# A hybrid diffusion step on one core: key halves copied by DMA, prompt steps and the last query turn moved, two small loads issued elsewhere

## The chip, the core and the metric

The kernel runs on one core of one Trainium2 chip. It is one program with five instruction streams: TensorE (PE, with its weight loads as PEld), VectorE (DVE), ScalarE (ACT), GpSimd (POOL) and SyncE (SP), which only issues DMAs here; ACT issues some DMAs too. Each stream runs in its own order, and streams wait for each other by semaphores. The metric is the device time of the program in microseconds, the median of several runs.

## The reference

One inference step of a two-layer trunk on 512 latent tokens and 128 prompt tokens of width 1024. Layer 0 mixes tokens by neighbourhood attention (16 heads, a bias table for each head), layer 1 by grouped-query attention (16 query heads, 4 key heads). Each layer ends in a gated feed-forward part with a convolution over three tokens. Cut to what matters here:

```python
qs, ks_, vs = na_qkv(hs, na_w_qkv[i])                       # layer 0
os_ = neighbourhood_attention(qs, ks_, vs, cache_na_k[:, i], cache_na_v[:, i], na_rpb[i])
...
qp, kp, vp = gqa_qkv(hp, gqa_w_qkv[i], gqa_q_norm[i], gqa_k_norm[i])   # layer 1, prompt
op = blocked_attention(qp, kp, vp)
qs, ks_, vs = gqa_qkv(hs, gqa_w_qkv[i], gqa_q_norm[i], gqa_k_norm[i])  # layer 1, latents
qs = axial_rope(qs); ks_ = axial_rope(ks_)
k_all = jnp.concatenate([ks_, cache_gqa_k[:, i]], axis=1)
os_ = blocked_attention(qs, k_all, v_all)
...
m = jax.nn.silu(cond) @ w + b                               # adaln: six rows for each layer
xs = xs + g_as * rmsnorm(os_ @ w_o, norm_mix_post[l])
fs = conv_ffn(hs, ffn_w_up[l], ffn_conv_w[l], ffn_conv_b[l], ffn_w_down[l])
```

## The kernel before

All matrices are fp32 and are split into a high and a low part (`wh`, `wl` for weights), and a product is three passes over them. Layer 0's attention runs from about 40 to 345 us of the span, its feed-forward part to 822, layer 1's key, query and attention stages to 1053, and its output projection and feed-forward part to the end at 1562. The order of all work is written out by hand, by lists of steps and tables of numbers; each engine's stream follows from the order in which the code issues.

**Layer 0.** A head's scores need a table `tb` of biases, made by three subtractions on POOL (L927) from `tr`, which three DMAs (L785, `na_runs`) fill. `tr` has one buffer for all heads but head 1. Tables 0 and 1 are loaded by SP; from table 2 (the third, h == 2) on ACT issues the DMAs, and those of table 2 are ordered behind a key cast (`kput`). POOL also normalises the probabilities `p` (L970) and makes the low parts `wl` of weights (L180). PE turns `p` (tile `tp`).

**Layer 1, keys and queries.** Five tiles of keys and values come first, then two rounds (hq 0, 1) of five query tiles of 24 matmuls each (`gp`). A key tile `kt` is normalised and rotated on DVE and POOL, turned on PE, and written by `turn_k` into `kh` (tile gkh, ACT L1558) and `kl` (tile gkl, DVE L1560). Both halves of the 128 partitions hold the same keys: the own half, and the other half, so that one matmul takes a query's high part against one and its low part against the other. A query tile is turned two tiles after its products (`tq`) and written by `turn_q` into `gq` (ACT L1572, DVE L1573).

**Prompt steps.** The prompt's attention of key heads 0 and 1 (a and b) has three steps each: scores (`sp`), turns, values. `PSTEP` lists after which query tile i (0 to 9) a step is taken from the list `extra`, in the order a0 a1 a2 b0 b1 b2.

**Units.** The latents' attention is 32 units. A unit's two scores (`s`) are two double-width PSUM tiles; DVE takes the row extremum `nmg` (L1687), ACT the exponential `gp` (L1688), DVE a reciprocal, POOL the scaling, PE the turns (`tp`). Units 0 and 1 are scored ahead, and then unit u+2 while unit u is turned. In between stands `mod_row`, the late row: 64 matmuls (tile `ada`) for one adaLN row of layer 1, an addition of its bias (tile `ax`, DVE L1821, loaded by two DMAs of SP at L1815), and a store (ACT, L1824). The last two query turns are taken from `extra` after that, the first at u == 0, the rest with the prompt steps from u == 6 (`PU0`).

Of the kernel before, what the change touches and what calls it, by code (L numbers as in the profile page):

```python
# [10 lines left out]
F32 = mybir.dt.float32  # L11
# [45 lines left out]
    "p0 s0 s1 t0 f f f t1 f t2 f s2 p1 f s3 v p2 f f f f".split(),  # L57
)
PRO = 20
PSTEP = (3, 5, 6, 6, 8, 9)  # L60
WU = 29
TP = 1
PSN = 4
# [41 lines left out]
def hybrid_step(ctx: ExitStack, tc: tile.TileContext, A, O):  # L105
# [19 lines left out]
    def f32(t):  # L125
        return t.bitcast(F32)
# [350 lines left out]
    vpool = l_na.enter_context(pool("nav", 3))  # L477
    tpool = l_na.enter_context(pool("nat"))
    mask = tpool.tile([P, 2, 32, 8], F32, name="mask")
    kput = []  # L480
    wqkv = A["na_w_qkv"][0]

    def na_v_tile():
# [289 lines left out]
    with l_na:  # L773
# [3 lines left out]
        def na_runs(h, q=nc.scalar):  # L777
            if h == 1:
                tr = wp.tile([P, 2, RUN], F32, tag="wr", name="tr")
            else:  # L780
                tr = tpool.tile([P, 2, RUN], F32, tag="tr", name="tr", bufs=1)
            runs[h] = tr
            base = h * RLEN + RPAD
            for dst, off, n in ((tr[:, 0, :], -8, 16), (tr[0:64, 1, :], 8, 8), (tr[64:128, 1, :], -16, 8)):
                i = q.dma_start(dst, raw_ap(A["k_rpb"], base + off, [[1, n], [31, 8], [1, RUN]]))  # L785
                if h == 2:
                    behind(i, kput[0])
            return i

        tbs = [ap.tile([P, 7, P], F32, name=f"tb{i}", bufs=1) for i in range(2)]  # L790
# [35 lines left out]
        def na_qk_items(p):  # L826
# [10 lines left out]
            def load_k():  # L837
                d["wk"] = wsplit(rows(wqkv, 0, 8, 1024 + P * p, P), 8, P, nc.gpsimd if p else None, high=kput if p == 2 else None)
                if not p:
                    nc.sync.dma_start(mask, A["k_mask"])  # L840
                    for h in range(2):
                        i = na_runs(h, nc.sync)
                    queue.extend([i] * 3)

            def k_put(c0, c1, src):
                for b in range(2):
# [72 lines left out]
        def na_table(h):  # L919
            if h not in runs:  # L920
                na_runs(h)
            tr = runs.pop(h)
            tb = tbs[h % 2]
            for w, dst in ((1, tb[:, 0::6, :]), (0, tb[:, 1:3, :]), (0, tb[:, 4:6, :])):
                t0 = tr[:, w, :]
                rv = raw_ap(t0, RUN - 1, [t0.ap[0], [-16, 2], [-1, 16], [-31, 8]])
                nc.gpsimd.tensor_sub(  # L927
                    dst.rearrange("p c (a b) -> p c a b", b=8),
                    mask[:, w].rearrange("p (c a) b -> p c a b", c=2), rv,
                )  # L930
            return tb

        class Head:
# [18 lines left out]
            def scores(self, slot):  # L952
                b, nm, su, rc = self.b, self.nm, self.su, self.rc
                qs, kh, kl = qk_of[self.h // 2]
                sp = bk.get("s")
                lq = qs[b][:, slot * P : slot * P + P]
                s3 = sp[:, 0:384].rearrange("p (a b) -> p a b", b=P)
                mm(s3, lq, keys(kh[b], slot), start=True, stop=False)
                mm(s3, lq, keys(kl[b], slot), start=False, stop=True)
                pt = ap.tile([P, 384], F32, tag="p", name="p", bufs=NPT)  # L960
                self.pts.append(pt)
                nc.vector.tensor_tensor_reduce(
                    s3, s3, self.tb[:, self.TABLE[slot], :],
                    1.0, BIG, ALU.add, ALU.min, nm[:, slot : slot + 1],
                )
                nc.scalar.activation(pt, sp[:, 0:384], AF.Exp, bias=nm[:, slot : slot + 1],
                                     scale=-1.0, accum_out=su[:, slot : slot + 1])
                bk.put(sp)
                nc.vector.reciprocal(rc[:, slot : slot + 1], su[:, slot : slot + 1])
                nc.gpsimd.tensor_scalar(pt, pt, rc[:, slot : slot + 1], 1.0, op0=ALU.mult, op1=ALU.mult)  # L970

            def turns(self, i):
                tp = bk.get("tp")
# [575 lines left out]
    def turn_k(src, cols):  # L1549

        tp = bk.get("tk")
        for j in range(2):
            turn(tp[:, j * P : j * P + P], src[:, j * P : j * P + P], ident)
        tv = tp[:, 0:256].rearrange("p (a b) -> p a b", a=2)
        for b in range(2):
            own, oth = own_oth(b)
            for part in (own, oth):
                nc.scalar.copy(kh[part, b::2, cols], tv[own])  # L1558
            for part in (own, oth):
                nc.vector.tensor_sub(kl[part, b::2, cols], tv[own], f32(kh[own, b::2, cols]))  # L1560
        bk.put(tp)

    def turn_q(src, hq, t):
# [168 lines left out]

    ck = ap.tile([P, 256], F32, tag="ck", name="ck", bufs=1)
    nc.scalar.dma_start(ck, A["cache_gqa_k"][0, 0].rearrange("t h d -> t (h d)"))
    cv = ap.tile([P, 256], F32, tag="cv", name="cv", bufs=1)
    nc.scalar.dma_start(cv, A["cache_gqa_v"][0, 0].rearrange("t h d -> t (h d)"))
    norms, turns = deque(), deque()

# [29 lines left out]
    for t in range(NT):  # L1768
        step(kv_tile(t, wkv, t == 0, queries(t)), KP[t])
        if t == 0:  # L1770
            late[0]()
        elif t == 1:
            late[1]()
            xmp.close()
            wx_s = ExitStack()
            wx = wx_s.enter_context(pool("wx", 2))
            pp_s = ExitStack()
            cur = [pp_s.enter_context(pool("prp", 1))]
    turns.append(lambda: turn_k(ck, slice(NS, T)))
    put_v(5, cv)  # L1780
    extra, ada_raws = deque(), []
    for hq in range(2):
        for n, t in enumerate(((4, 0, 1, 2, 3), (0, 1, 2, 3, 4))[hq]):
            if hq and n == PSN:
# [6 lines left out]
                    k = len(ada_raws) - 1  # L1791
                    nc.sync.dma_start(ada_raws[k], A["ada_w"][1, k * P : k * P + P, 3 * D : 4 * D])
            if n == 2:
                extra.extend(gqa_prompt(2 * hq) + gqa_prompt(2 * hq + 1))
            for _ in range(PSTEP.count(i)):
                extra.popleft()()
    turns.append(norms.popleft()())
    extra.extendleft(reversed(turns))
    pp_s.close()
    wx_s.close()  # L1800
    hp2.close()
# [4 lines left out]
    with ExitStack() as s:  # L1806
        ap = s.enter_context(pool("ga", 2, "right"))
        cur = [ap]
        def mod_row():

            l, idx = 1, 3
            x = ap.tile([P, 256], F32, name="ax", bufs=1)
            nc.gpsimd.memset(x, 0.0)
            for q in range(2):
                nc.sync.dma_start(x[q::32, :], A["ada_b"][l, idx * D : idx * D + D].rearrange("(j c) -> j c", j=4))  # L1815
            ps = bk.get("ada")
            for k, raw in enumerate(ada_raws):
                for j in range(4):
                    mm(ps[32 * j : 32 * j + 32, 0:256], scolp[:, 2 * k : 2 * k + 32], raw[:, 256 * j : 256 * j + 256],
                       start=k == 0, stop=k == KC - 1)  # L1820
            nc.vector.tensor_add(x, ps[:, 0:256], x)  # L1821
            bk.put(ps)
            for q in range(2):
                nc.scalar.dma_start(modrow[l][idx][q].rearrange("(j c) -> j c", j=4), x[q::32, :])  # L1824

        m1 = Mix(1, A["gqa_w_o"][0], lambda p, t: tuple(x[:, t * P : t * P + P] for x in osp1[p]))

# [1 line left out]
        un[1] = Unit(1)  # L1829
        for i in range(2):  # L1830
            un[1].scores(i)
        mod_row()
        for u in range(NU + 2):
            if u + 2 < NU:
                un[u + 2] = Unit(u + 2)
            for step in GORDER[u % 2]:
                if step == "p":
                    if extra and (u == 0 or u >= PU0):
                        extra.popleft()()
                elif step[0] == "s" and u + 2 < NU:  # L1840
                    un[u + 2].scores(int(step[1]))
# [115 lines left out]
```

## Time and profile before

| | us |
|---|---|
| median of three runs | 1566.82 (1566.13 to 1567.01) |
| the profiled execution | 1564.15 |
| its span, first to last instruction | 1562.4 |
| busy: PE, DVE, ACT, POOL | 1518.7, 1028.1, 858.4, 700.2 |
| mean granted clock of TensorE | 0.996 |

A row of a timeline gives the start in us of the span, the time, the engine, the line of the kernel, the operation, output tile and input tiles, and how many instructions the row holds. In brackets stands how long the engine was idle ahead of it, and which instruction ended that. `SPq` and `ACTq` are the DMA queues of those engines: the time is that of the issue. A row of a table of windows gives the stretch, its length, the busy time of PE, PEld, DVE, ACT and POOL with counts, PE's clock, the busy share of the DMA engines and GB/s.

### The profile page before, as it was taken

What the parts mean: (1) busy time and instruction counts of PE and PEld (TensorE: products, weight loads), DVE (VectorE), ACT (ScalarE), POOL (GpSimd) and SP (SyncE); (2) the same over time, 40 slices, a digit from 0 to 9 for tenths busy, and PEclk for the clock granted to TensorE, in tenths of its full rate; (3) what the DMA queues carried; (4) which work ended last, traced back from release to release, by engine and by line L of the source; (5) the groups of instructions that cost most, each with busy time, mean ns of one, the idle gap of its engine ahead of it and who ended that gap; (6) DMA issues with size and microseconds to landing.
All of it is one profiled execution on the core that took longest, in us unless ns stands there. A gap on an engine that the chain in (4) does not pass through costs nothing.

```text
span 1562.4 us, 26067 instructions
## 1 busy us (share of the span) xinstructions
PE 1518.7 (97%) x9709; PEld 1347.9 (86%) x9709; DVE 1028.1 (66%) x1660; ACT 858.4 (55%) x1636; POOL 700.2 (45%) x606
## 2 busy tenths in 40 slices
PE   6999999999999999999999989999999999999998
PEld 5988998788999999988887767878899999988886
DVE  4543443659877666765747877772988887886554
ACT  5664664646655555554545446772666665554443
POOL 1555554432355455534544454541325666552433
PEclk9999999999999999999999999999999999999999
DMA  9745454253565664478574221005533335447664
GB/s 326 191 124 146 131 135 115 63 186 125 181 223 180 221 190 151 138 253 280 185 223 149 77 69 41 1 2 190 187 104 115 115 108 157 129 157 264 218 222 134
DMA packets 193210, 242.41 MB, mean 155 GB/s; under 512 B 11100, under 2 KB 149564, under 8 KB 193084
## 3 DMA queue, kind: packets, MB, share of 16 engines
q1 hardware_dynamic: 182944, 233.91, 46.5%
q10 hardware_dynamic: 10140, 6.85, 2.5%
q8 instruction: 76, 1.25, 0.3%
q14 instruction: 50, 0.41, 0.1%
HBM read 214.38 MB, written 26.34 MB: 154 GB/s over the span
## 4 chain that ended last, share of the span: by engine, by line
PE 62%; DVE 7%; ACT 2%; issue 2%; POOL 2%; DMA 2%; ACTq 0%; POOLq 0%; DVEq 0%; SPq 0%
PE acc L117 19%; PE ux L117 18%; PE uz L117 8%; PE uy L117 4%; PE y L117 2%; PE po L117 2%; PE s L117 2%; PE tp L120 2%; PE gp L117 2%; PE ada L117 1%; DMA wr<-in_ffn_w_up 1%; DVE wl L180 1%; DVE t L1277 1%; DMA gn<-in_gqa_k_norm 1%; DVE gkl L1560 1%
## 5 line engine op out<-in xcount | busy, mean ns | idle before, releaser
L180 POOL TENSOR_TENSOR wl<-wr,wh 128x1024 fp32r<-128x1024 f32 x70 | 173.3, 2479 | 239.7 <-ACT wh L178 228.7
L1200 POOL TENSOR_TENSOR wl<-wr,wh 128x1024 fp32r<-128x1024 f32 x76 | 183.5, 2435 | 48.3 <-ACT wh L1199 44.7
L117 PE MATMUL ux<-B,wh 128*128 128x322 f32 x832 | 200.1, 311 | 0.9 <-ACT u L1254 0.9
L1277 DVE SCALAR_TENSOR_TENSOR t<-C,cw,t 128x644 f32<-128x644 f32 x176 | 156.4, 888 | 51.3 <-ACT t L1275 50.7
L178 ACT CAST wh<-wr 128x1024 fp32r<-128x1024 f32 x140 | 145.5, 1048 | 51.1 <-DMA wr<-in_ffn_w_down 36.7
L117 PE MATMUL acc<-wh,alo 128*128 128x512 f32 x440 | 172.3, 392 | 0.3 <-DVE alo L1169 0.3
L117 PE MATMUL acc<-wl,ahi 128*128 128x512 f32 x440 | 172.0, 391 | 0.0
L117 PE MATMUL acc<-wh,ahi 128*128 128x512 f32 x440 | 171.9, 391 | 0.0
L117 PE MATMUL uz<-B,wh 128*128 128x322 f32 x640 | 156.1, 312 | 1.5 <-ACT v L1254 1.5
L117 PEld LDWEIGHTS ux<-B,wh 128*128 128x128 f32 x832 | 143.6, 189 | 3.4 <-ACT u L1254 1.6
L1169 DVE TENSOR_TENSOR alo<-ain,ahi 128x384 fp32r<-128x384 f32 (+1 forms) x88 | 81.5, 946 | 87.7 <-ACT ahi L1167 86.7
L117 PE MATMUL ux<-B,wl 128*128 128x322 f32 x416 | 129.5, 311 | 2.6 <-DVE wl L1200 2.6
L117 PE MATMUL qk<-hT,wh 128*128 128x384 f32 (+1 forms) x512 | 123.0, 316 | 0.0
L117 PEld LDWEIGHTS uz<-B,wh 128*128 128x128 f32 x640 | 110.9, 189 | 4.9 <-ACT v L1254 2.0
L1200 POOL TENSOR_TENSOR vl<-wr,vh 128x1024 fp32r<-128x1024 f32 x38 | 95.9, 2523 | 24.6 <-ACT vh L1199 24.3
L1199 ACT CAST wh<-wr 128x1024 fp32r<-128x1024 f32 x84 | 84.8, 1048 | 40.0 <-DVE wr L1223 39.6
L1275 ACT ACTIVATE t<-C,cw 128x644 f32<-128x644 f32 x88 | 78.6, 893 | 48.3 <-DVE C L1305 40.7
L180 DVE TENSOR_TENSOR wl<-wr,wh 128x1024 fp32r<-128x1024 f32 x70 | 90.7, 1306 | 20.8 <-ACT wh L178 20.2
L117 PE MATMUL uz<-B,wl 128*128 128x322 f32 x320 | 99.6, 311 | 0.3 <-POOL wl L1200 0.3
L117 PEld LDWEIGHTS acc<-wh,alo 128*128 128x128 f32 x440 | 82.6, 188 | 18.8 <-DVE alo L1169 1.1
L117 PEld LDWEIGHTS acc<-wl,ahi 128*128 128x128 f32 x440 | 82.6, 188 | 18.2 <-POOL wl L180 0.3
L117 PEld LDWEIGHTS acc<-wh,ahi 128*128 128x128 f32 x440 | 82.5, 188 | 17.7
(259 smaller groups left out, 3878.1 us busy)
## 6 DMA issues: line engine op xcount, KB each, us to landing
wr<-in_ffn_w_up SPq DMA_DIRECT2D x88, 512.0 KB
wr<-in_ffn_w_down SPq DMA_DIRECT2D x88, 512.0 KB
wr<-in_ada_w SPq DMA_DIRECT2D x72, 512.0 KB
act<-act SPq DMA_DIRECT2D x44, 321.0 KB
wr<-in_na_w_qkv SPq DMA_DIRECT2D x24, 512.0 KB
mod<-modrow SPq DMA_DIRECT2D x20, 512.0 KB
ain<-act SPq DMA_DIRECT2D x44, 192.0 KB
wf<-in_ada_w SPq DMA_DIRECT2D x16, 512.0 KB
```

The source lines that it names most:

```text
L117: pe(nc.tensor.matmul(*a, **k))
L120: pe(nc.tensor.transpose(*a, **k))
L178: i = nc.scalar.copy(hi, raw)
L180: j = (low or nc.vector).tensor_sub(lo, raw, f32(hi))
L1169: pin(nc.vector.tensor_sub(lo[:, 0 : c1 - c0], ain[:, 0 : c1 - c0], f32(hi[:, 0 : c1 - c0])))
L1199: nc.scalar.copy(hl[0], src)
L1200: low.tensor_sub(hl[1], src, f32(hl[0]))
L1275: nc.scalar.activation(t, taps(0), AF.Identity, bias=cw[:, 3, n : n + 1], scale=cw[:, 1, n : n + 1])
L1277: nc.vector.scalar_tensor_tensor(t, taps(d), cw[:, w, n : n + 1], t, op0=ALU.mult, op1=ALU.add)
L1560: nc.vector.tensor_sub(kl[part, b::2, cols], tv[own], f32(kh[own, b::2, cols]))
```

## The change

Four parts.

1. `turn_k`: ACT and DVE write only the own half of `kh` and `kl`; the other half is copied from it by 24 DMAs of SP, each of 64 partitions x 2 x 128. The tile `cv` moves to the buffers of `kt`, and its use to the second key tile.
2. The prompt steps: `PSTEP` changes, and so does the order of steps.
3. The late row: its tile is cleared and its bias loaded before the query tiles, and its store moves from ACT to SP. The last query norm is taken after unit 1's scores, and no step is taken at u == 0.
4. Table 2: its three DMAs are issued by SP in `load_k` of the second head pair, and its subtractions are ordered behind head 0's last normalisation.

```diff
-PSTEP = (3, 5, 6, 6, 8, 9)
+PSTEP = (4, 6, 6, 7, 8, 9)
...
     def na_runs(h, q=nc.scalar):
...
                 i = q.dma_start(dst, raw_ap(A["k_rpb"], base + off, [[1, n], [31, 8], [1, RUN]]))
-                if h == 2:
-                    behind(i, kput[0])
...
             def load_k():
...
+                if p == 1:
+                    na_runs(2, nc.sync)
...
         def na_table(h):
...
-                nc.gpsimd.tensor_sub(
+                i = nc.gpsimd.tensor_sub(
...
+                if h == 2:
+                    behind(i, plast[0])
...
-                nc.gpsimd.tensor_scalar(pt, pt, rc[:, slot : slot + 1], 1.0, op0=ALU.mult, op1=ALU.mult)
+                i = nc.gpsimd.tensor_scalar(pt, pt, rc[:, slot : slot + 1], 1.0, op0=ALU.mult, op1=ALU.mult)
+                if not self.h:
+                    plast[:] = [i]
...
     def turn_k(src, cols):
...
-            for part in (own, oth):
-                nc.scalar.copy(kh[part, b::2, cols], tv[own])
-            for part in (own, oth):
-                nc.vector.tensor_sub(kl[part, b::2, cols], tv[own], f32(kh[own, b::2, cols]))
+            nc.scalar.copy(kh[own, b::2, cols], tv[own])
+            nc.vector.tensor_sub(kl[own, b::2, cols], tv[own], f32(kh[own, b::2, cols]))
+            for k in (kh, kl):
+                nc.sync.dma_start(f32(k[oth, b::2, cols]), f32(k[own, b::2, cols]))
...
-    cv = ap.tile([P, 256], F32, tag="cv", name="cv", bufs=1)
+    cv = ap.tile([P, 256], F32, tag="kt", name="cv", bufs=3)
...
+    ada_x = kp.tile([P, 256], F32, name="ax")
+    nc.gpsimd.memset(ada_x, 0.0)
+    for q in range(2):
+        nc.sync.dma_start(ada_x[q::32, :], A["ada_b"][1, 3 * D : 4 * D].rearrange("(j c) -> j c", j=4))
     for hq in range(2):
...
-                extra.extend(gqa_prompt(2 * hq) + gqa_prompt(2 * hq + 1))
+                a, b = gqa_prompt(2 * hq), gqa_prompt(2 * hq + 1)
+                extra.extend((a[0], a[1], b[0], a[2], b[1], b[2]))
...
-    turns.append(norms.popleft()())
-    extra.extendleft(reversed(turns))
...
         def mod_row():
...
-            x = ap.tile([P, 256], F32, name="ax", bufs=1)
-            nc.gpsimd.memset(x, 0.0)
-            for q in range(2):
-                nc.sync.dma_start(x[q::32, :], A["ada_b"][l, idx * D : idx * D + D].rearrange("(j c) -> j c", j=4))
...
-                nc.scalar.dma_start(modrow[l][idx][q].rearrange("(j c) -> j c", j=4), x[q::32, :])
+                nc.sync.dma_start(modrow[l][idx][q].rearrange("(j c) -> j c", j=4), x[q::32, :])
...
             un[1].scores(i)
+        turns.append(norms.popleft()())
+        extra.extendleft(reversed(turns))
         mod_row()
...
                 if step == "p":
-                    if extra and (u == 0 or u >= PU0):
+                    if extra and u >= PU0:
                         extra.popleft()()
```

Three places in the engines' streams follow: a row has the line, the operation, output and input tiles with the output's shape, and in brackets the engines or DMA semaphores for which it waits. Line numbers of the changed kernel differ by a few. The first place is SP's stream at the weights of the third head pair, before:

```order
L293 DMA wr<-in_ada_w 128x1024 [waits DMAHW7_49]
L174 DMA wr<-in_na_w_qkv 128x8x128 [waits DMAHW1_49,DVE_49]
L309 DMA abias<-in_ada_b 4x256 [waits DMAHW2_49,Pool_49]
L311 DMA again<-in_norm_mix_post 4x256 [waits DMAHW3_49,Pool_49]
L309 DMA abias<-in_ada_b 4x256 [waits DMAHW4_49]
```

and now:

```order
L293 DMA wr<-in_ada_w 128x1024 [waits DMAHW7_49]
L785 DMA tr<-in_k_rpb 128x1x249 [waits DMAHW5_49,DMAHW1_49,Pool_49]
L785 DMA tr<-in_k_rpb 64x1x249 [waits DMAHW2_49]
L785 DMA tr<-in_k_rpb 64x1x249 [waits DMAHW3_49]
L174 DMA wr<-in_na_w_qkv 128x8x128 [waits DMAHW4_49,DVE_49]
L309 DMA abias<-in_ada_b 4x256 [waits DMAHW5_49]
L311 DMA again<-in_norm_mix_post 4x256 [waits DMAHW6_49]
```

The three DMAs of table 2 now stand in SP's stream, ahead of the third pair's first weight load. The second place is PE's stream at the first prompt score, before, with the end of the fourth query tile's products, its turns, and the scores:

```order
L117 MATMUL gp<-wl,hT_7810 128x512
L117 MATMUL gp<-wh,hT_7811 128x512
L120 MATMUL tq<-ident,qt 128x128 [waits DVE_49,PE_49]
L120 MATMUL tq<-ident,qt 128x128 x3
L117 MATMUL sp<-gkh,gq_9263 128x128 [waits DVE_49]
L117 MATMUL sp<-gkl,gq_9263 128x128
L117 MATMUL sp<-gkh,gq_9263 128x128
L117 MATMUL sp<-gkl,gq_9263 128x128
L117 MATMUL sp<-gkh,gq_9264 128x128 [waits DVE_49,PE_49]
```

and now, one query tile further on:

```order
L117 MATMUL gp<-wl,hT_7810 128x512
L117 MATMUL gp<-wh,hT_7811 128x512
L120 MATMUL tq<-ident,qt 128x128 [waits DVE_49,PE_49]
L120 MATMUL tq<-ident,qt 128x128 x3
L117 MATMUL sp<-gkh,gq_9263 128x128 [waits DMAHW2_49,Activation_49]
L117 MATMUL sp<-gkl,gq_9263 128x128 [waits DMAHW3_49]
L117 MATMUL sp<-gkh,gq_9263 128x128
L117 MATMUL sp<-gkl,gq_9263 128x128
L117 MATMUL sp<-gkh,gq_9264 128x128 [waits DVE_49,PE_49]
```

The scores moved behind 24 more products and four more turns, and wait for two of the copies. The third place is DVE's stream at the late row, before:

```order
L1573 TENSOR_TENSOR gq_9265<-tq,gq_9265 64x4x128 [waits Activation_49]
L1544 TENSOR_TENSOR qt<-qt,rh 128x512 [waits DVE_49,Pool_49]
L1687 TENSOR_REDUCE nmg<-s_10262 128x1 [waits PE_49]
L1573 TENSOR_TENSOR gq_9266<-tq,gq_9266 64x4x128 [waits Activation_49]
L1687 TENSOR_REDUCE nmg<-s_10271 128x1 [waits PE_49]
L1690 RECIPROCAL rcg<-sug 128x1 [waits Activation_49]
L1821 TENSOR_TENSOR ax<-ada,ax 128x256 [waits DMAHW4_49,DMAHW5_49,PE_49,Pool_49]
L1690 RECIPROCAL rcg<-sug 128x1 [waits Activation_49]
L1687 TENSOR_REDUCE nmg<-s_10324 128x1 [waits PE_49]
```

and now:

```order
L1577 TENSOR_TENSOR gq_9265<-tq,gq_9265 64x4x128 [waits Activation_49]
L1691 TENSOR_REDUCE nmg<-s_10265 128x1 [waits PE_49]
L1577 TENSOR_TENSOR gq_9266<-tq,gq_9266 64x4x128 [waits Activation_49]
L1691 TENSOR_REDUCE nmg<-s_10274 128x1 [waits PE_49]
L1694 RECIPROCAL rcg<-sug 128x1 [waits Activation_49]
L1548 TENSOR_TENSOR qt<-qt,rh 128x512 [waits DVE_49,Pool_49]
L1694 RECIPROCAL rcg<-sug 128x1 [waits Activation_49]
L1824 TENSOR_TENSOR ax<-ada,ax 128x256 [waits PE_49]
L1691 TENSOR_REDUCE nmg<-s_10324 128x1 [waits PE_49]
```

The last query norm (`qt`) moved behind both maxima of unit 1, and the late row's addition waits for PE alone. Key copies in SP's stream: three stand ahead of the first, and ten ahead of the second, of the last two weight loads for the queries, and all 24 ahead of the loads for the late row's 64 matmuls.

More of the change, by code (lines that the diff above doesn't have):

```diff
@@ L479, in hybrid_step @@
     mask = tpool.tile([P, 2, 32, 8], F32, name="mask")
-    kput = []
+    kput, plast = [], []
     wqkv = A["na_w_qkv"][0]
@@ L1772, in hybrid_step @@
         elif t == 1:
+            put_v(5, cv)
             late[1]()
@@ L1809, in mod_row @@
         def mod_row():
-            l, idx = 1, 3
-            x = ap.tile([P, 256], F32, name="ax", bufs=1)
-            nc.gpsimd.memset(x, 0.0)
-            for q in range(2):
-                nc.sync.dma_start(x[q::32, :], A["ada_b"][l, idx * D : idx * D + D].rearrange("(j c) -> j c", j=4))
+            l, idx, x = 1, 3, ada_x
             ps = bk.get("ada")
```

1 line of the change is left out of this document (removed).

## The prediction

> **What bounds the kernel now.** I read the busy shares first, then TensorE's list of waits, then the timeline around each long wait, and last the granted clock in short windows.
>
> ```profile
> PE 1518.7 (97%) x9709; PEld 1347.9 (86%) x9709; DVE 1028.1 (66%) x1660; ACT 858.4 (55%) x1636; POOL 700.2 (45%) x606
> ...
> PE s L117 <- ACT gp L1688: 6.0, 9, 3.1
> PE tp L120 <- POOL p L970: 4.5, 5, 2.9
> ...
> PE sp L117 <- DVE gq L1573: 3.0, 2, 1.9
> PE ux L117 <- DVE wl L1200: 2.6, 2, 1.3
> ...
> PE tp L120 <- DVE gq L1573: 1.2, 1, 1.2
> ```
>
> PE is busy for 97% of 1562.4 us, so 43.7 us of idle time is nearly all that a reordering can win; no matmul is removed. The columns of the waits are total, times, longest. Four of the five shown name the places that the change touches; ux belongs to the feed-forward part.
>
> **The third score table.** Views: timelines of POOL, ACT, SP and PE, and a window of PE's clock.
>
> ```profile
> 52.06 0.39 SPq L174 DMA_DIRECT2D wr<-in_na_w_qkv  x1
> ...
> 67.52 1.05 ACT L178 CAST wh<-wr 128x1024 fp32r<-128x1024 f32 x1
> ...
> 72.10 0.68 ACTq L785 DMA_DIRECT2D tr<-in_k_rpb  x1
> ...
> 73.61 0.62 ACTq L785 DMA_DIRECT2D tr<-in_k_rpb  x1
> ...
> 82.45 1.87 ACTq L785 DMA_DIRECT2D tr<-in_k_rpb  x3
> ...
> 73.40 2.28 POOL L970 TENSOR_SCALAR p<-p,rc 128x384 f32<-128x384 f32 x4
> 77.55 1.72 POOL L927 TENSOR_TENSOR tb<-mask,tr 128x256 f32<-128x256 f32 x2 [1.87 <-DMA tr<-in_k_rpb]
> ...
> 81.57 0.85 POOL L927 TENSOR_TENSOR tb<-mask,tr 128x256 f32<-128x256 f32 x1
> ...
> 90.41 2.53 POOL L927 TENSOR_TENSOR tb<-mask,tr 128x256 f32<-128x256 f32 x3 [6.85 <-DMA tr<-in_k_rpb]
> 92.90 2.34 POOL L180 TENSOR_TENSOR wl<-wr,wh 128x1024 fp32r<-128x1024 f32 x1
> 95.21 1.15 POOL L970 TENSOR_SCALAR p<-p,rc 128x384 f32<-128x384 f32 x2
> ...
> 95.85 1.03 PE L120 MATMUL tp<-ident,p 128*128 128x128 f32 x2 [2.94 <-POOL p L970]
> ...
> 95.85:99.15 3.30, 3.21 (x10) 2.92 (x11) 1.66 (x6) 2.73 (x11) 1.88 (x3) 0.50 0.86 198
> ```
>
> Read it backwards. PE stood 2.94 us for p, and then ran 3.30 us at clock 0.50. POOL reached p only at 95.21 because the fourth table (90.41) stood 6.85 us for its DMA. That DMA was issued at 82.45, as soon as the one `tr` buffer came free with the last subtraction of the third table (81.57 + 0.85 = 82.42). The third table was late because its own data, issued on ACT from 72.10, landed at 77.55. SyncE now issues these three DMAs about 54, 18 us sooner. The subtractions then follow p's x4 at 75.68 and end about 78.2 (three of 0.85); the fourth table's DMAs can go out from 78.2 in place of 82.45. ACT's casts stand between them, so I put the last at 82. The old ones took 90.41 - 84.32 = 6.1 us from the end of the last issue, with weights among them; the third table's took 77.55 - 74.23 = 3.3. Landing is 85.3 to 88.1. Then table 2.53, wl 2.34, first p 0.58: p at 90.8 to 93.6, against PE's need at 95.85 - 2.94 = 92.91. Between these I go by the third table's landing, since the new DMAs leave before the weights that the old ones met the stall goes: 2.94 plus half of the slow 3.21, together **4.5 us**; bounds 0 and 4.6.
>
> What the three DMAs push back on SP: the next weight load, 52.06 before, goes out about 4 us later (SP waits for table 1's subtractions to free `tr`, then three issues). Its cast stands at 67.52, over 15 us behind the old issue, so I cost it at nothing; without that cover it would be those 4 us.
>
> **The prompt scores.** Timelines of PE and DVE, and one window.
>
> ```profile
> 879.83 0.33 PE L117 MATMUL sp<-gkh,gq 128*128 128x128 f32 x1 [1.12 <-DVE gq L1573]
> ...
> 882.39 0.30 PE L117 MATMUL sp<-gkh,gq 128*128 128x128 f32 x1 [1.90 <-DVE gq L1573]
> ...
> 888.49 0.60 PE L120 MATMUL tq<-ident,qt 128*128 128x128 f32 x4
> ...
> 881.55 0.69 DVE L1573 TENSOR_TENSOR gq<-tq,gq 64x512 fp32r<-64x512 f32 x1
> ...
> 880.00:885.00 5.00, 3.10 (x17) 2.60 (x18) 4.05 (x9) 1.45 (x3) 2.66 (x4) 1.00 0.01 3
> ```
>
> The scores waited 1.12 and 1.90 us for the query halves, which DVE finished at 882.24. One query tile takes 5.6 us (from the last score, 882.9, to 888.49). With that tile put ahead, the scores start about 884.8, 2.5 us after the halves are there. The clock stayed 1.00 through both gaps, so the gain is **3.0 us** and no more; bounds 0 and 3.0. The steps behind it each move by a tile or less, past work that had no wait.
>
> **Key halves by DMA.** Groups of the tiles gkh and gkl (minimum/median/maximum ns), SP's and ACT's timelines.
>
> ```profile
> L1558 ACT CAST gkh<-tk x24: 352/367/370, 849.4 to 874.6; 64x256 fp32r<-64x256 f32 x24
> L1560 DVE TENSOR_TENSOR gkl<-tk,gkh x24: 402/422/428, 854.3 to 876.4; 64x256 fp32r<-64x256 f32 x24
> ...
> 856.39 2.57 SPq L174 DMA_DIRECT2D wr<-in_gqa_w_qkv  x2
> ...
> 888.50 2.00 ACT L178 CAST wh<-wr 128x1024 fp32r<-128x1024 f32 x2
> ```
>
> Removed: 12 x 0.367 = 4.4 us of ACT and 12 x 0.422 = 5.1 us of DVE between 849 and 877. PE did not wait for either in that stretch beyond the prompt scores, so it is worth nothing by itself; it makes the halves at 881.55 come a little sooner. Added: 24 DMAs of 64 KB on SP, some 0.6 us of issue each by the `tr` rows (15 us in all, spread over 20). The two weight loads of 856.39 now stand behind three and ten of them, and each copy waits for its cast, so the second load slips some 4 us; its cast comes at 888.50. Free. The copies that the first score needs come from the last key turn, whose last subtraction started at 876.4 (now sooner, with half the work ahead of it). With its 0.42, 0.6 of issue and 3.3 to 5.5 us for landing, as the third table's data took (from the end of the last issue, or from the first, to 77.55), they are there by 881 to 883, before 884.8. Free, with a margin of 2 us.
>
> [...]
>
> **The late row.** Timelines of PE, DVE and ACT, and one window.
>
> ```profile
> 929.23 0.56 PE L117 MATMUL s<-gkh,gq 128*128 128x320 f32 x2 [0.84 <-ACT gp L1688]
> ...
> 929.92 0.60 PE L120 MATMUL tq<-ident,qt 128*128 128x128 f32 x4
> ...
> 935.18 0.72 PE L117 MATMUL s<-gkh,gq 128*128 128x320 f32 x2 [3.08 <-ACT gp L1688]
> ...
> 938.88 1.08 PE L120 MATMUL tp<-ident,gp 128*128 128x128 f32 x4 [1.17 <-DVE gq L1573]
> ...
> 941.97 0.67 PE L117 MATMUL s<-gkh,gq 128*128 128x320 f32 x2
> ...
> 926.74 0.78 DVE L1544 TENSOR_TENSOR qt<-qt,rh 128x512 f32<-128x512 f32 x1 [0.73 <-POOL rh L1522]
> 927.45 0.81 DVE L1687 TENSOR_REDUCE nmg<-s 128x1 f32<-128x640 f32 x1
> ...
> 932.59 0.42 DVE L1821 TENSOR_TENSOR ax<-ada,ax 128x256 f32<-128x256 f32 x1 [2.56 <-DMA ax<-in_ada_b]
> ...
> 933.00 1.53 DVE L1687 TENSOR_REDUCE nmg<-s 128x1 f32<-128x640 f32 x2
> ...
> 928.29 0.79 ACT L1688 ACTIVATE gp<-s,nmg 128x640 f32<-128x640 f32 x1 [1.67 <-DVE nmg L1687]
> ...
> 934.24 0.79 ACT L1688 ACTIVATE gp<-s,nmg 128x640 f32<-128x640 f32 x1 [3.48 <-DVE nmg L1687]
> ...
> 935.50:942.00 6.50, 5.33 (x25) 4.88 (x23) 3.99 (x8) 3.73 (x10) 2.31 (x3) 0.50 0.49 160
> ```
>
> DVE stood 2.56 us for two small DMAs, with the row maxima of the next two scores behind it (933.00), ACT's exponentials behind those (934.24), and PE behind these (3.08). Loaded ahead, that wait is gone. Also the last query norm (926.74, with its 0.73) no longer stands before the maximum of 927.45. New chain: maximum at 926.0 (926.74 less the idle 0.73), exponential 926.8; the next maximum, behind a gq half of 0.69, 927.5 to 928.3, exponential to 929.3; reciprocals, the norm (0.78) and the row (0.42) till 929.8; maximum till 930.6; exponential till 931.6. PE's score of 935.18 then starts about 931.8, after 1.2 us of idle instead of 3.08. From there to 941.97 PE took 6.8 us, of it 1.17 idle and the rest at clock 0.50; at full clock that is 2.8, with 0.4 for a wait left over 3.2. So 941.97 becomes 935.0, 7.0 us less, but the four turns of 929.92 (0.60) now come later, with perhaps 0.4 for a new wait there: **6.0 us**. Upper bound: all idle, 0.84 + 3.08 + 1.17 = 5.1, and half of 5.33, 7.8. Lower bound: only the 2.56 of DVE comes off and the slow clock stays, 2.6.
>
> [...]
>
> **Sum.** 4.5 + 3.0 + 6.0 = 13.5 us, with the copies, the early clearing and loading of the row and its store on SP at zero. The profiled execution took 1564.15 us, so 1550.65 for such a one; it lies 2.67 below the median of 1566.82, and against the median it is **1553.3**.
>
> **Rivals.**
> 1. *The fourth table stays late*: its DMAs meet the weight load at 82 as before, and POOL reaches p no sooner. For it: 6.1 us of landing. Against: two of three are out before that load. The 4.5 go: 1557.8.
> 2. *The late row is only half cured*: the chain maximum, exponential, score keeps a gap near 3 us and the clock falls all the same. For it: each link is 0.8 to 1.0 us and four follow each other; against: 1.3 us of slack over what I need. It wins 2.6: 1556.7; together with 1, 1561.
> 3. *Slower: the copies go one after another.* Place: SP's queue and the DMA engines, 855 to 885; PE's first prompt score waits for the 22nd copy. Price by the `tr` rows: 5.45/3 = 1.82 us each if only throughput binds, so from the first subtraction on 854.3 + 40 = 894.3, a stall of 9.5 at 884.8, and 1.7 of slow clock (as at 95.85): 1564.5, no change. At 3.3 us each (one landing after another) 926.9, a stall of 42: 1597. It is slower than before by more than 0.2% from 2.1 us per copy on. [...]
> 4. *Nothing arrives at the end*: a load or a vector chain after 1053 sets the end. Against: PE's longest wait there is 1.3 us. 1563 to 1567.
>
> **How the numbers follow.** Forecast (1549.5 to 1556) 0.64; rivals 1 and 2, one or both (1556 to 1561), 0.23; rival 4, 0.08; rival 3, 0.05. A change of under 0.2% (3.1 us) is about what cannot be told from none here. Faster: 0.64 + 0.23 and a part of rival 4, 0.89; same 0.07; slower 0.04 (rival 3 above 2.0 us). The range takes the upper bounds (4.6 + 3.0 + 7.8, and 1.9 for what the freed DVE and ACT time may add) as its low end, 1549.5, and rivals 1 and 2 together as its high end, 1561; left out are rivals 3 and 4, 0.13.
>
> **What would show it.** Right: the wait of tp for p under 1 us in all; no window at 0.50 near 96 or 936; sp without a wait; DVE's `ax` addition without a DMA before it. Wrong: sp or s waiting for a DMA, SP's copies landing after 884, wh of the query weights waiting for a DMA, or a new wait of PE for tq between 885 and 930.

## The result and the profile after

The changed kernel takes 1548.82 us (median of four runs, 1547.69 to 1550.43) against 1566.91: ratio 0.9878, interval 0.9862 to 0.9895, 18.1 us less. (The ratios further on leave out one execution, of the version of experiment 4 with an own buffer in before, that took 5273 us.) The forecast was 1553.3 in 1549.5 to 1561.0, so the gain was larger than forecast and the time just below the range. The two profiled executions lie 1564.15 - 1550.43 = 13.7 us apart, close to the 13.5 of the sum. So the question is not what the change did in that execution, but why the medians lie further apart than the executions that were profiled.

The changed kernel's page and list of TensorE's waits (total, times, longest):

```profile
PE 1513.5 (98%) x9709; PEld 1343.4 (87%) x9709; DVE 1022.3 (66%) x1648; ACT 854.0 (55%) x1624; POOL 702.2 (45%) x606
...
PE s L117 <- ACT gp L1692: 3.2, 8, 0.9
PE ux L117 <- DVE wl L1204: 3.0, 2, 1.7
PE tp L120 <- POOL p L972: 1.6, 4, 0.9
```

The waits for gq are gone, the others at the three places are under 1 us each. (The 1.6 us of tp for p are short waits near 76 us and one of 0.9 at 292; none is left near 94.) Its timelines of SP, ACT, POOL and PE at the fourth score table:

```profile
54.62 2.72 SPq L785 DMA_DIRECT2D tr<-in_k_rpb  x3
...
82.34 0.62 ACTq L785 DMA_DIRECT2D tr<-in_k_rpb  x1
...
76.65 2.54 POOL L927 TENSOR_TENSOR tb<-mask,tr 128x256 f32<-128x256 f32 x3
...
87.63 2.56 POOL L927 TENSOR_TENSOR tb<-mask,tr 128x256 f32<-128x256 f32 x3 [4.97 <-DMA tr<-in_k_rpb]
...
92.52 1.15 POOL L972 TENSOR_SCALAR p<-p,rc 128x384 f32<-128x384 f32 x2
...
93.83 0.60 PE L120 MATMUL tp<-ident,p 128*128 128x128 f32 x4
```

Table 2's data is there when POOL comes to it, table 3 (the fourth) starts at 87.63 instead of 90.41, p is ready before PE comes. The last DMA landed 87.63 - 82.96 = 4.7 us after the end of its issue (82.34 + 0.62), between the two ends that I had. At the prompt scores (SP, PE) and at the late row (DVE, PE), and in three windows of the clock:

```profile
869.35 0.59 SPq L1564 DMA_DIRECT2D gkl<-gkl  x1
...
881.05 0.31 PE L117 MATMUL sp<-gkh,gq 128*128 128x128 f32 x1
...
922.57 0.40 DVE L1824 TENSOR_TENSOR ax<-ada,ax 128x256 f32<-128x256 f32 x1
922.89 1.54 DVE L1691 TENSOR_REDUCE nmg<-s 128x1 f32<-128x640 f32 x2
...
924.74 0.56 PE L117 MATMUL s<-gkh,gq 128*128 128x320 f32 x2 [0.94 <-ACT gp L1692]
...
927.69 0.54 PE L117 MATMUL s<-gkh,gq 128*128 128x320 f32 x2
...
92.00:96.00 4.00, 4.00 (x26) 3.95 (x25) 2.07 (x6) 3.19 (x12) 2.61 (x4) 1.00 0.74 126
880.50:885.50 5.00, 5.00 (x29) 4.25 (x28) 4.87 (x11) 1.06 (x2) 1.54 (x2) 1.00 0.80 248
921.00:928.50 7.50, 6.31 (x54) 5.19 (x42) 6.21 (x14) 4.99 (x12) 6.05 (x11) 1.00 0.12 27
```

The copies are all issued 11 us before the first score; DVE's addition has no bracket, so it waits for nothing; the score behind it waits 0.94. The clock (the last figure but two) is 1.00 at all three places.

### The profile page after: what moved, and what is told of

Its sections match the earlier page's. It is cut to its first block, busy times and chain, and to the rows that moved or that the text cites. A ratio compares the mean times of both kernels' runs of the same rounds, so it can differ in the third digit from the quotient of the medians.

```text
span 1548.6 us, 26098 instructions
## 1 busy us (share of the span) xinstructions
PE 1513.5 (98%) x9709; PEld 1343.4 (87%) x9709; DVE 1022.3 (66%) x1648; ACT 854.0 (55%) x1624; POOL 702.2 (45%) x606
## 4 chain that ended last, share of the span: by engine, by line
PE 63%; DVE 5%; ACT 2%; issue 2%; POOL 2%; DMA 1%; POOLq 0%; DVEq 0%; ACTq 0%
PE ux L117 18%; PE acc L117 17%; PE uz L117 8%; PE gp L117 5%; PE uy L117 4%; PE po L117 3%; PE y L117 2%; PE s L117 2%; PE tp L120 2%; PE ada L117 1%; DMA wr<-in_ffn_w_down 1%; DVE t L1281 1%; POOL wl L180 1%; DMA wr<-in_ffn_w_up 1%; DVE wl L180 1%
```

## The experiments

All runs are set against the kernel before on the same chip; the interval of a ratio is about 0.0015 to each side, 2.3 us. A time is compared with that of the changed kernel measured beside it where there is one, and otherwise ratio with ratio (the changed kernel's is 0.9873 to 0.9884).

**1. Both kernels again, unchanged.**

> The kernel before, unchanged, run again. Open is why the medians lie 18.1 us apart (1566.91 and 1548.82) where the profiled executions lie 13.7 apart (1564.15 and 1550.43). Theory A, the places are the same in every execution and only the start and the clock windows vary: this run's stages from the first qk matmul on lie within 1 us of the profiled execution of before, its start within 2 us, and any time beyond that stands in one or two more stretches at clock 0.50 (1.7 us for each 3.4 us stretch); ratio 1.000, times 1564 to 1569. Theory B, the profiled execution of before was a lucky one and a typical one has a further wait of 2 to 4 us in one of the three places of the change: then that wait shows here, over 2 us longer than in the profiled execution of before.

> The changed kernel, unchanged, run again. In its profiled execution the start ran 1.3 us later than in before (first qk 0.54, qk 200 1.30 later). Theory A, this is chance of the start: here the start lies anywhere from 1.5 us earlier to 1.3 later, the rest as in the profiled execution of after; times 1547.5 to 1550.5, ratio 0.986 to 0.990. Rival: the three loads put into SyncE's queue at 54 us delay the weights of the third head pair and so PE's start every time: then qk 200 is again 1 us or more later than in before, and the loss is part of the change.

Before: 1567.44, ratio 1.0002. Changed: 1549.60, ratio 0.9884 (0.9869 to 0.9899), and once more 1547.79, ratio 0.9873 (0.9857 to 0.9890):

> The changed kernel again, as the measure for the three others of this call: 1548 to 1550, clock 0.998 or 0.999 in every execution.

Theory A holds for the three places. The profiled execution of before was an uncommonly fast one; the second, at 1570.58 us, is one of the slowest. In it (list of waits, timeline and windows of PE) the waits at the three places are nearly the same, but not the clock, and there is one wait for wl, at 1464 us, that the first lacks:

```profile
PE acc L117 <- POOL wl L180: 1.3, 1, 1.3
...
880.67 0.33 PE L117 MATMUL sp<-gkh,gq 128*128 128x128 f32 x1 [1.15 <-DVE gq L1573]
883.23 0.44 PE L117 MATMUL sp<-gkh,gq 128*128 128x128 f32 x1 [1.90 <-DVE gq L1573]
...
95.20:102.50 7.30, 7.22 (x33) 6.83 (x34) 4.15 (x11) 5.16 (x15) 5.09 (x5) 0.58 0.41 96
...
882.00:890.50 8.50, 7.27 (x21) 5.92 (x22) 6.30 (x15) 4.72 (x13) 3.83 (x4) 0.60 0.01 3
...
938.00:950.00 12.00, 9.80 (x49) 7.93 (x50) 6.54 (x14) 6.69 (x15) 3.73 (x5) 0.59 0.30 96
```

The 1.90 us gap before the prompt scores, after which I had seen the clock stay at 1.00, is now followed by a stretch at half clock of 6.8 us; the stretch after p is 6.8 instead of 3.4, that after the late row 10.2 instead of 6.8. The wait for wl stands in four other profiles too (1.1 to 1.4 us), all of versions of the changed kernel, and with 0.5 us, at 1444, in the changed kernel's first; it goes with neither kernel.

Every execution of these runs has its mean clock on record. Over 78 executions of before it is 0.9936 on average (0.990 to 0.996; only two reached the 0.996 of the profiled one), over 12 of the changed kernel 0.9985 (all 0.998 or 0.999). (1 - clock) x span adds up the clock that was missing, as time at full speed: 10.1 us and 2.3 us, 7.8 apart. For the two profiled executions the same figures are 6.2 and 3.1, 3.1 apart, each to within 0.8 us, since the clock is on record to three places. The difference of 4.7 us is close to what the medians have more than the profiled pair (18.1 - 13.7 = 4.4).

That does not show that all of the 4.4 us is clock, for (1 - clock) x span counts more than the clock cost here. Between the two profiles of before it differs by 7.9 us (14.1 and 6.2), but PE was busy only 4.2 us longer, for the same matmuls (1518.7 in the first; here the second):

```profile
PE 1522.9 (97%) x9709; PEld 1350.0 (86%) x9709; DVE 1033.3 (66%) x1660; ACT 858.5 (55%) x1636; POOL 701.0 (45%) x606
```

Over the 78 executions the time rises by 0.9 us for each 0.001 of clock that is missing, where the whole span would give 1.6. And the changed kernel's first profiled execution was a slow one of its kind, 1.6 us above its median, with a start 1.3 us late. So half clock is a part of the 4.4 us, and chance at the start is likely another; how they divide is not shown. The second pair of profiled executions lies 20.6 us apart (1570.58 and 1549.99), so that single pairs lie on both sides of 18.1.

The start is chance as well: the matmul that stood 1.3 us late in the first profile of the changed kernel stands 0.36 late in its second, though the first PE instruction was 0.84 late. The rival of a loss through SP's queue falls; in its third profile that matmul is 0.56 early.

**2. The score table alone.** Undone in the changed kernel (first diff), and done alone in before:

```diff
-                if p == 1:
-                    na_runs(2, nc.sync)
+                if h == 2:
+                    behind(i, kput[0])      # in na_runs, on ACT
...
-                if h == 2:
-                    behind(i, plast[0])     # in na_table
```

> The changed kernel with the third score table loaded by ACT behind the key cast again, as before; all else as changed. My theory: TensorE's wait for p of 2.9 us near 95 us and the half clock behind it come back, 4.5 us slower than the changed kernel (about 1553.3, ratio to before 0.991). Rival: the wait comes back but without the half clock, 2.9 us (1551.7). Rival: the gain of this part is small, since the start is faster without the three loads in SyncE's queue by 1 us: 3.5 us.

> The kernel before with only the third score table loaded by SyncE. Theory A: TensorE's wait for p of 2.9 to 3.3 us goes, with one or two stretches of 3.4 us at half clock: 4 to 6 us faster than before. Rival B: the three loads in SyncE's queue cost up to 1 us at the start: 3 to 4 us faster.

Undone: 1552.83, ratio 0.9911 (0.9897 to 0.9924), 3.2 us over the changed kernel beside it by medians, 4.2 by ratios. The wait is back:

```profile
PE tp L120 <- POOL p L970: 4.0, 4, 2.7
```

with 3.4 us of half clock, which decides against the rival without it; the times alone would not. Done alone: 1561.37 against 1567.84, ratio 0.9961 (0.9949 to 0.9974), 6 us faster, within theory A. The term of 4.5 lies between.

**3. Keys and prompt steps.**

```diff
-PSTEP = (4, 6, 6, 7, 8, 9)
+PSTEP = (3, 5, 6, 6, 8, 9)
...
-                extra.extend((a[0], a[1], b[0], a[2], b[1], b[2]))
+                extra.extend(gqa_prompt(2 * hq) + gqa_prompt(2 * hq + 1))
```

> The changed kernel with the prompt steps where and in which order they stood before (the first scores one query tile sooner); the key halves still go by DMA. My theory: the first prompt scores wait again for the query halves, 2 to 3 us in two waits, less by what the freed DVE saves (up to 1 us); so 2 to 3 us slower than the changed kernel, 1551 to 1552. Rival: they now wait for the last copies (issued till about 870 and landed 3.3 to 5.5 us later, 874 to 876, PE there at 875): up to 1 us, a wait named by a DMA. Rival: the freed DVE is enough and the step could have stayed: 0.

Measured 1549.02, ratio 0.9885: nothing lost. The scores do not wait at all; DVE, PE and SP:

```profile
873.36 0.69 DVE L1577 TENSOR_TENSOR gq<-tq,gq 64x512 fp32r<-64x512 f32 x1
...
874.13 0.31 PE L117 MATMUL sp<-gkh,gq 128*128 128x128 f32 x1
...
868.17 0.59 SPq L1564 DMA_DIRECT2D gkl<-gkl  x1
```

The halves are ready at 874.05, just ahead of the score, and the copies have landed too. The last rival was right: with the keys copied the step could have stayed. The other way round, both halves written by the engines again:

```diff
-            for k in (kh, kl):
-                nc.sync.dma_start(f32(k[oth, b::2, cols]), f32(k[own, b::2, cols]))
+            # for part in (own, oth): ACT copy and DVE subtraction, as before
```

> The changed kernel with both key halves written by ACT and DVE again, no copies; all else as changed. My theory: nothing, within 0.5 us of the changed kernel, since the scores stand one tile later and TensorE waits for neither engine there. Rival: the freed 4.4 us of ACT and 5.1 us of DVE are part of the gain beyond what I summed: 1 to 3 us slower, with waits of TensorE for gq, tq or gvt between 845 and 910. Rival the other way: the copies cost something in SyncE's queue and it is 1 us faster.

1551.52, ratio 0.9897 (0.9884 to 0.9911), some 2 to 3 us over the changed kernel, at the edge of what these intervals separate. Its profile shows no wait for gq, so the later step alone takes that wait away too. Two waits stand behind it that the changed kernel does not have, for POOL's pp (0.31) and for DVE's sq:

```profile
911.11 0.53 PE L117 MATMUL s<-gkh,gq 128*128 128x320 f32 x2 [0.68 <-DVE sq L1540]
```

So about 1 us of the loss is the engines' time, as the first rival had it, though not by the waits that it named; the place of the rest stays open. Both undone together, and the copies alone in before:

> The changed kernel with both the key copies and the prompt steps undone. Undone alone, the steps cost nothing and the keys at most 2 us. Theory A, either alone takes away the wait for the query halves: together the two waits (1.1 and 1.9 us) come back, and in part of the executions a stretch of half clock of 3.4 or 6.8 us behind them: 3 to 6.5 us slower than the changed kernel (1552.5 to 1556), clock 0.995 to 0.998 from one execution to the next. Rival B, as in the profiled execution of before the clock stays up: 3.0 us in all executions, clock 0.998 to 0.999.

> The kernel before with only the key halves copied by DMA; the prompt steps stay where they were, so the first score stands one tile earlier than in the changed kernel. Theory A: the freed DVE has the query halves ready, the two waits of 1.1 and 1.9 us go and with them the half clock that stands behind them in some executions: 3 to 6 us faster than before. Rival B: the scores wait for the last copies instead, within 1 us of before. Rival C, by the idle time alone: 3.0 us faster.

Both undone: 1554.82 against 1547.79 beside it, ratio 0.9922 (0.9908 to 0.9937), 7.0 us slower; clock 0.996 to 0.998. In its profile one gap of 1.90 us is enough for a stretch of 3.4 us at half clock (the window of 3.5 us holds 1.8 of it, at a mean of 0.74):

```profile
873.92 0.33 PE L117 MATMUL sp<-gkh,gq 128*128 128x128 f32 x1 [0.33 <-DVE gq L1577]
876.48 0.30 PE L117 MATMUL sp<-gkh,gq 128*128 128x128 f32 x1 [1.90 <-DVE gq L1577]
...
876.50:880.00 3.50, 3.50 (x14) 2.90 (x15) 3.40 (x9) 0.67 (x2) 2.77 (x3) 0.74 0.02 7
```

Copies alone: 1561.04 against 1567.84, ratio 0.9961 (0.9947 to 0.9974), 6 us faster, and no wait of the scores. Theory A at both ends, with 6 to 7 us at or just over the top of its ranges, where I had summed 3.0. Either part alone is enough to take the wait away: undone one by one they cost nothing and 2 to 3 us. This execution also shows the other side of chance, a gap that costs no clock:

```profile
96.05 0.33 PE L120 MATMUL tp<-ident,p 128*128 128x128 f32 x1 [2.88 <-POOL p L970]
...
96.00:99.50 3.50, 3.22 (x21) 2.99 (x22) 1.86 (x7) 3.03 (x13) 2.07 (x3) 1.00 0.84 197
```

Each copy twice:

```diff
-            for k in (kh, kl):
+            for k in (kh, kh, kl, kl):
```

> The changed kernel with each of the 24 key copies issued twice, 48 in all, doubling their cost in SyncE's queue and in the DMA engines. My theory: issues take 0.6 to 0.7 us each, so the last leaves some 8 to 14 us later (about 880 instead of 869.9) and the first prompt scores at 881 wait 2 to 5 us for it; the single copies have about 6 us to spare. [...] Rival, they are free even twice: 0.

1558.00, ratio 0.9931 (0.9917 to 0.9945), some 8.3 us over the changed kernel. PE's and SP's timelines:

```profile
884.72 0.45 PE L117 MATMUL sp<-gkh,gq 128*128 128x128 f32 x1 [4.61 <-DMA gkh<-gkh]
...
885.91 0.59 SPq L1564 DMA_DIRECT2D gkl<-gkl  x1
```

The 24 further copies put the last issue 885.91 - 869.35 = 16.6 us later, 0.69 us each (I had expected 8 to 14): the price is the issue, not a landing each. The wait is 4.6 us, with 6.8 us of half clock; it begins 2.1 us before the wait ends (first row, PE idle), and that part costs nothing:

```profile
882.60:884.72 2.12, 0.00 (x0) 0.03 (x1) 0.00 (x0) 0.00 (x0) 0.00 (x0) 0.50 0.53 102
884.72:889.40 4.68, 4.54 (x14) 3.87 (x15) 0.00 (x0) 0.00 (x0) 0.00 (x0) 0.50 0.77 176
```

At 2.1 us a copy, from which rival 3 would decide, the single copies would have been late; at 0.69 they are not.

**4. The late row.** First the load moved back in the code, and the turn alone moved back:

```diff
-    nc.gpsimd.memset(ada_x, 0.0)             # before the query tiles
-    ... dma_start(ada_x ...)
+            nc.gpsimd.memset(x, 0.0)         # in mod_row
+            ... dma_start(x ...)
```

> The changed kernel with the late row's clearing and bias load back at their old place in front of its matmuls; its store stays on SyncE and the last query turn stays later. My theory: DVE's addition waits for the DMA again (2.5 us), the two row maxima, the exponentials and the score behind it too; with over 3 us of idle PE the clock falls for one or two stretches: 4 to 6 us slower than the changed kernel (1553 to 1555). Rival: the earlier exponentials absorb a part, the gap stays under 2 us and the clock stays up: 1 to 2 us.

> The version with the late row's load at its old place once more, beside the changed kernel on the same chip: it was the fastest so far (1547.63). Theory: the load does not matter once the last query turn stands later, so the two are the same within 0.5 us. Rival: it is faster by 1 to 2 us, since two DMAs and a clearing less stand at 823 us.

```diff
-        turns.append(norms.popleft()())
-        extra.extendleft(reversed(turns))
         mod_row()
...
-                    if extra and u >= PU0:
+                    if extra and (u == 0 or u >= PU0):
```

> The changed kernel with the last query norm taken before the row maxima of unit 1 and the first of the last turns at u = 0 again; the late row stays loaded ahead. My theory: the maxima come 1.5 us later, the scores of units 2 and 3 wait 1 to 2 us more, no half clock: 1.0 to 2.5 us slower than the changed kernel. Rival: it is hidden, 0, since the load was the whole cause. Rival: idle of over 2 us is enough to let the clock fall: 3.5 to 5 us slower.

> The changed kernel with both halves of the late-row part undone: the bias loaded late, and the last query turn early with its step at u = 0. Undone one by one they cost nothing (load) and 1 to 2 us (turn). Theory A, either one alone cures the wait, since each takes one link out of the chain: undone together the wait of 3 us before a score comes back with one to three stretches at half clock, 6 to 9 us slower than the changed kernel (1556 to 1558), clock 0.995 to 0.997. Rival B, the two add up: 1 to 2 us slower, no stretch at half clock; then the late row was never the place where most of the gain came from.

Load moved back: 1547.63, ratio 0.9870 (0.9856 to 0.9883), and 1548.97 beside 1547.79: no difference that shows twice. Turn moved back: 1551.24, ratio 0.9894, 2.5 us by ratios and no half clock, as my theory had it. Both: 1552.02, ratio 0.9901 (0.9884 to 0.9918), 4.2 us slower than the changed kernel beside it, without a wait for the load or any half clock there. Theory A of that run fell: the wait did not come back, since these versions were not what they were meant to be. The tile kept a buffer of its own, and clearing and loads, put into the code late, were still issued early, at 819 us. In SP's stream there is no load near the row, and DVE (profile of both moved back) has no wait:

```profile
922.93 0.41 DVE L1826 TENSOR_TENSOR ax<-ada,ax 128x256 f32<-128x256 f32 x1
```

So the tile was put back into the attention stage's buffers, alone and with the early turn:

```diff
-    ada_x = kp.tile([P, 256], F32, name="ax")
+            x = ap.tile([P, 256], F32, name="ax", bufs=1)
```

> The changed kernel with the late row's tile taken again from the buffers of the attention stage (free only when the query stage gives them back) and loaded in front of its matmuls. In the earlier version the tile kept a buffer of its own, and its clearing and loads moved ahead to 823 us by themselves. Theory A, the buffer is what made the load late: DVE's addition waits for the DMA again (about 2.5 us), a score waits 2 to 3 us, with a stretch of half clock: 3 to 7 us slower than the changed kernel (1552 to 1556), clock 0.995 to 0.998. Rival B, with the last query turn later the load is hidden anyway: 0 to 1 us, no wait of DVE for it.

> The changed kernel with the late-row part undone in full: shared buffer, late load, last query turn early, a step at u = 0 (the store stays on SyncE). Theory A: the wait of about 3 us before a score and 6.8 or 10.2 us of half clock behind it are back, 7 to 9 us slower than the changed kernel (1556 to 1558), clock 0.994 to 0.997. Rival B: 4 us, as when the tile kept its own buffer.

1554.76, ratio 0.9923 (0.9908 to 0.9939), and 1554.62, ratio 0.9921 (0.9907 to 0.9936): 6.7 to 7 us slower than the changed kernel by ratios (0.9878). DVE and PE of the second:

```profile
924.98 0.42 DVE L1826 TENSOR_TENSOR ax<-ada,ax 128x256 f32<-128x256 f32 x1 [2.52 <-DMA ax<-in_ada_b]
...
927.23 0.83 PE L117 MATMUL s<-gkh,gq 128*128 128x320 f32 x2 [2.70 <-ACT gp L1692]
```

Theory A: the buffer made the load late (in the first of the two the score waits 4.2 us for the same reason). With the buffer shared, the turn adds nothing. From the side of before, each edit alone:

> The kernel before with one thing changed: the late row's tile has a buffer of its own (and cv shares that of kt, to make room), the code of its load stays where it was. Theory A: clearing and loads move ahead by themselves, DVE does not wait for a DMA, the score's wait of 3.1 us falls under 1 us and its half clock goes: 4 to 7 us faster than before (1560 to 1563). Rival B: the store on ACT between the exponentials still holds the chain, and it gains under 2 us.

> The kernel before with only the last query turn later and no step at u = 0. Theory A: the load stays late, the score's wait is still 2 to 3 us and the half clock stays: 0 to 2 us faster than before. Rival B: a link less in the chain is enough to bring the wait under 2 us: 4 to 6 us faster.

Own buffer: ratio 0.9988 (0.9978 to 0.9999), 1.9 us. Turn later: 0.9994 (0.9984 to 1.0005), nothing that can be told, as theory A of the turn had it. Theory A of the buffer does not hold; the gain is that of its rival B. With the buffer alone the wait goes to the turned query (first line, PE), which still drew 3.4 us of half clock; with the turn alone the load comes no sooner (issued at 934.3, where before had 930.0 with PE 4.3 us earlier), PE reaches the score sooner, and the score waits 4.4 us (second line, the list of waits):

```profile
938.64 1.09 PE L120 MATMUL tp<-ident,gp 128*128 128x128 f32 x4 [2.01 <-DVE gq L1573]
...
PE s L117 <- ACT gp L1688: 7.0, 8, 4.4
```

So in before neither is enough alone: each leaves one gap of 2 us or more there (2.01 and 4.4), and half clock behind it; the mean clock of the two profiled executions is 0.995 and 0.992. The changed kernel with the turn alone moved back has the same early turn and an early load, and there the largest gap is 1.08 us and the clock stays up (mean 0.999 in its profiled execution). At this place the two differ by the store. In before with its own buffer (first two rows, ACT) the cast of the turned query stands behind the row's stores; in the changed kernel with the early turn (last two, ACT and PE) the store is on SP, and the cast comes 1.9 us sooner, counted from the start of the second unit's exponential (932.29 and 921.28):

```profile
933.36 0.49 ACTq L1825 DMA_DIRECT2D modrow<-ax  x1
...
934.98 0.56 ACT L1572 CAST gq<-tq 64x512 fp32r<-64x512 f32 x1
...
922.07 0.56 ACT L1576 CAST gq<-tq 64x512 fp32r<-64x512 f32 x1
...
926.71 0.63 PE L120 MATMUL tp<-ident,gp 128*128 128x128 f32 x4 [1.08 <-DVE gq L1577]
```

That is the place that rival B of the buffer named. No run moves the store alone, so its worth in time is not shown; the rows show only where it stood.

## Why the prediction was too small, and where its mechanism held

Undone one at a time in the changed kernel, the three places cost 3.2 to 4.2, 7.0 and 6.7 to 7.0 us, each to within some 2 us, together 17 to 18 of the 18.1 us. Against the forecast's 4.5, 3.0 and 6.0 it is the second term that is clearly mis-sized.

- *The score table, 4.5.* In the profiled pair PE goes from 1.3 us late (qk's 200th matmul) to 3.2 early: 4.5. By undoing and doing alone 3 to 6 us. The step held, and the weight load pushed back in SP's queue (57.43 for 52.06, 5.4 us where I said 4) cost nothing.
- *The prompt scores, 3.0.* Here the prediction failed: "The clock stayed 1.00 through both gaps, so the gain is 3.0 us and no more". It was one execution's luck. In six profiled executions with that gap the clock fell in five. Measured, with the copies: 6 to 7 us, and the upper bound of 3.0 too low by 3 to 4. The cause was also put in one part alone: the later step does take the wait away, but with the copies it was not needed.
- *The key copies, 0 by themselves.* Wrong: they made the halves sooner, which I named and did not count, and alone in before they gained 6 us. That PE waits for neither engine "beyond the prompt scores" held in before; with the scores moved and the engines writing both halves it waits 0.68 us for DVE behind them, and the copies are worth 2 to 3 us. The cover for SP's queue and the landing held.
- *The late row, 6.0.* The chain came out as worked: addition done at 922.97, score at 924.74, the later score at 927.69; with PE 6.9 us ahead by then these are 929.9, 931.7 and 934.6 in before's time (forecast 929.8, 931.8, 935.0). The gain there is 7.4 us where 7.0 was forecast, and the one us that I had charged for the moved turns was not spent: 7.1 are left at the end of the attention stage. By undoing, 6.7 to 7. The store, put at zero, may have had a share, which no run separates.
- *The sum against the median.* I noted that the profiled execution lay 2.67 below the median and carried that over as a constant. It was in part half clock missing from that execution, and the change takes half clock away: before has 10.1 us of it on average, not 6.2, which is more than its cost in time. The late start of the changed kernel's profiled execution is likely another part of the 4.4 us. How they divide is not shown.
- *The idle time.* The 43.7 us of idle time were not "nearly all that a reordering can win": half clock stands in the busy time. In the profiled pair PE's busy time fell by 5.2 us (1518.7 to 1513.5) with the same 9709 matmuls.
- *Rivals.* 1 and 2 did not come: the fourth table was there in time (p ready at 93.1, so near the late end of what I had worked out), and no gap near 3 us was left. 3: issued twice, the copies took 0.69 us each, not 2.1, and their issues follow each other at 0.6 to 0.7 us; more than that they did not cost. No run shows the 2.0 us a copy from which the prediction put its chance of a slower kernel. 4: the gain arrived at the end, 13.75 of 14.0 us in the profiled pair.

## What to carry to other kernels

A short gap of TensorE cost its length here and, by chance, a stretch at half clock behind it (3.4 to 10.2 us at 19 of 21 places with gaps of 1.9 to 4.6 us), so price a gap with the mean clock of many executions, not with the one that was profiled: (1 - mean clock) x span adds up the clock that was missing; less than that came back in time (0.9 us for each 0.001 of clock, where the whole span would give 1.6). If the profiled execution is faster than the median, look for what it happened to miss before you carry the difference over, and profile a second one. The late row's load was as early as its buffer was free: with a buffer of its own it went out early, at 819 us, though its line stood late in the code, and with a shared buffer the same line made it late, at 922 and 925.

## What the runs showed of the hardware that was not expected

In the 20 traces 21 places behind the first 50 us had gaps of PE with a longest one of 1.9 to 4.6 us. At 19 the clock went to half, for 3.4, 6.8 or 10.2 us, beginning between 2.5 us ahead of the gap's end and 1.9 us behind it; at two (1.90 and 2.88 us) it stayed at full speed. At lone gaps of 0.9 to 1.75 us between there and the last matmuls it never fell. In the first 50 us, where short gaps stand closer together, eight traces have a stretch too (seven of 3.4 us from about 19 us on, one of 10.2 from 26) though no gap between matmuls there is over 1.6 us, and twelve with much the same gaps have none. A gap of 1.90 us was followed by nothing, 3.4 or 6.8 us, one of 4.08 by 3.4: the length of the gap did not set the loss, and 1.9 us was enough for half clock to follow.
